# Moving the store of batch 28 behind the last load in a streaming mixture of softmaxes

## Chip, cores, metric

One core of a Trainium2 chip. DVE is the vector engine (VectorE), ACT the scalar engine (ScalarE); SP (SyncE) issues the large transfers, and the DMA engines carry them out. The metric is the device time of one execution in microseconds (us); the number of a kernel is the median of its runs. A profiled run also has a "span", from its first to its last instruction, which is about 1.8 us shorter than the device time; times inside a trace count from the start of the span.

## The reference

Logits are [32 batches, 128 rows, 4 heads, 4096], all float32: 268 MB in, 67 MB out.

```python
prior_probs = softmax(prior, axis=-1)              # [32, 128, 4]
softmax     = softmax(logits, axis=-1)             # over the 4096 entries
mixture     = np.sum(prior_probs[..., None] * softmax, axis=2)
```

## The kernel before

One batch is 8 MB of logits, held in one of two `ltile` buffers. ACT takes the exponential of each head and its row sum; DVE turns the sum into a coefficient and scales or accumulates. The result is 2 MB per batch. It lies in one of two `acc` buffers, and for batches 30 and 31 in the logits' own tile. Batches 30 and 31 are loaded in four pieces, one per head; the last batch is stored in two halves.

```python
    def load(b):
        lt = lpool.tile([P, H, V], FP32, name="ltile")       # two buffers
        n = pieces(b)                                        # 1 for b >= 30, else 4
        for h in range(0, H, n):
            nc.sync.dma_start(out=lt[:, h : h + n], in_=logits[b, :, h : h + n, :])
        ltiles[b] = lt

    def store(b, lo=0, hi=V):
        nc.sync.dma_start(out=out[b, :, lo:hi], in_=accs[b][:, lo:hi])
    # ... load(0), load(1); prior to probabilities: small, at the start ...
    for b in range(B):
        last = b == B - 1
        inplace = b >= B - 2
        # ... lt, acc ...
        for h in range(H):
            split = last and h == H - 1
            et = lt[:, h] if inplace else epool.tile([P, V], FP32, name="etile")
            nc.scalar.activation(et, lt[:, h], AF.Exp, accum_out=dsum)        # L98
            nc.vector.reciprocal(rden, dsum)                                  # L101
            nc.vector.tensor_mul(coeff, rden, pp[:, h, b : b + 1])            # L102
            if h == 0:
                nc.vector.tensor_scalar_mul(out=acc, in0=et, scalar1=coeff)   # L104
            elif not split:
                nc.vector.scalar_tensor_tensor(                               # L106
                    out=acc, in0=et, scalar=coeff, in1=acc, op0=ALU.mult, op1=ALU.add)
            else:
                ...  # last head of batch 31: four quarters (L112), a half store after two
        if b + 2 < B:
            load(b + 2)
        if not last:
            store(b)
```

All these transfers are issued by SP, in this order, into one queue. For the end that is: load 29, store 27, load 30, store 28, load 31, store 29, store 30, two halves of store 31.

The softmax here doesn't subtract the row's maximum and nothing guards it: scores larger than these inputs give would overflow.

## Time and profile before

| | before |
|---|---|
| device time, median of the first 3 runs | 785.83 us (784.52 to 786.05) |
| span of the profiled run | 783.7 us |
| bytes moved | 335.68 MB, 428 GB/s over the span |
| DVE, ACT busy | 70%, 60% |

The DMA-issuing queue of SP, kernel before, from 705 us on (start, duration, what):

```profile
710.70 1.80 SPq L45 DMA_DIRECT2D ltile<-in_logits_dram  x4
716.47 0.34 SPq L51 DMA_DIRECT2D out_dram<-acc  x1
734.89 1.79 SPq L45 DMA_DIRECT2D ltile<-in_logits_dram  x4
740.66 0.34 SPq L51 DMA_DIRECT2D out_dram<-acc  x1
757.68 19.31 SPq L51 DMA_DIRECT2D out_dram<-ltile  x3
```

These are load 30, store 28, load 31, store 29, and then three stores merged into one line. So store 28 is ahead of load 31 and store 29 already is behind it.

DVE in batch 31, kernel before (start, duration, what; in brackets the idle time before and what ended it):

```profile
757.95 2.35 DVE L104 TENSOR_SCALAR ltile<-ltile,coeff 128x4096 f32<-128x4096 f32 x1
761.52 0.16 DVE L101 RECIPROCAL rden<-dsum 128x1 f32<-128x1 f32 x1 [1.22 <-ACT ltile L98]
...
771.75 4.87 DVE L112 SCALAR_TENSOR_TENSOR ltile<-ltile,coeff 128x1024 f32<-128x1024 f32 x4
```

DVE waits 1.22 us in this batch, for an exponential that itself waited for its piece of load 31, and ends at 776.62.

The same kernel at its end, in windows of 2 us (columns: window, length, busy us of DVE, ACT and POOL, TensorE clock, DMA share, GB/s; a packet counts in the window where it starts, so a full window can read a little over 1):

```profile
768.00:770.00 2.00, 2.00 (x1) 2.00 (x1) 0.00 (x0) 1.00 0.96 410
770.00:772.00 2.00, 1.93 (x4) 1.33 (x2) 0.00 (x0) 1.00 1.03 442
772.00:774.00 2.00, 2.00 (x2) 0.00 (x0) 0.00 (x0) 1.00 0.58 246
774.00:776.00 2.00, 2.00 (x3) 0.00 (x0) 0.00 (x0) 1.00 0.63 262
776.00:778.00 2.00, 0.63 (x1) 0.00 (x0) 0.00 (x0) 1.00 1.02 422
778.00:780.00 2.00, 0.00 (x0) 0.00 (x0) 0.00 (x0) 1.00 1.00 418
```

There is a hole in the DMA share between 772 and 776 us, and this is what a reordering would hope to fill.

One more reading needs the packet and completion records. Every large transfer has 16 completions, one from each DMA engine (the records do not say which; that it is the same engine that comes last each time is inferred from its lag, which stays the same from one transfer to the next for long stretches). In this run the first of them and the last lie 4.2 us apart for load 29 (714.53 and 718.74). The Trainium skill, "DMA: Bandwidth & Descriptors", section "Why a DMA increments its semaphore by 16 and not by 1", says that the engines of one DMA finish independently and that only the full count means that all data has landed; the trace agrees, with that 4.2 us. So the DMA share is a mean over 16 engines that are not at the same place in the queue.

### The profile page before, as it was taken

The numbers are of one execution on the slowest core, as the hardware profiler recorded it, in microseconds if no ns is written. First come the engines' busy times: TensorE is split into PE (matmuls) and PEld (weight loads), VectorE is DVE, ScalarE is ACT, GpSimd is POOL, SyncE is SP. The second block draws the span as 40 slices with busy tenths as digits, with TensorE's granted clock in tenths as the row PEclk, the third lists the DMA queues.
The fourth block names the chain that finished last, engine by engine and source line by source line (L and its number), as shares of the span: only waits on it lengthen the run. The fifth ranks groups of instructions, "written<-read, shape, count | busy, mean of one in ns | idle before, by whom it ended". The sixth has DMA issues, their size and how long they took to land.

```text
span 783.7 us, 1001 instructions
## 1 busy us (share of the span) xinstructions
DVE 547.5 (70%) x408; ACT 472.7 (60%) x258; POOL 0.2 (0%) x4
## 2 busy tenths in 40 slices
DVE  3588568766687666786666866668756687666996
ACT  0776555775557755567555576555765557755963
POOL 0000000000000000000000000000000000000000
DMA  9999999999999999999999999999999999999997
GB/s 378 428 462 421 438 429 399 457 428 428 428 425 436 451 445 435 420 421 447 429 428 425 431 456 442 435 428 404 456 432 428 428 429 438 458 432 403 430 430 317
DMA packets 10280, 335.68 MB, mean 428 GB/s; under 512 B 1152, under 2 KB 1152, under 8 KB 1184
## 3 DMA queue, kind: packets, MB, share of 16 engines
q1 hardware_dynamic: 10224, 335.55, 99.4%
q10 hardware_dynamic: 48, 0.07, 0.0%
q14 instruction: 8, 0.07, 0.0%
HBM read 268.50 MB, written 67.11 MB: 428 GB/s over the span
## 4 chain that ended last, share of the span: by engine, by line
DMA 66%; ACT 14%; DVE 12%; issue 6%; DVEq 0%; SPq 0%; ACTq 0%
DMA ltile<-in_logits_dram 62%; ACT etile L98 14%; DVE acc L106 10%; DMA out_dram<-acc 4%; DVE ltile L106 1%; DVE rden L101 1%; ACT ltile L98 0%; DVE ltile L112 0%; DVE coeff L102 0%; DVE acc L104 0%; DVEq L147 0%; SPq L45 0%; ACTq L98 0%; DVEq L104 0%
## 5 line engine op out<-in xcount | busy, mean ns | idle before, releaser
L98 ACT ACTIVATE etile<-ltile 128x4096 f32<-128x4096 f32 x120 | 433.4, 3612 | 280.0 <-DMA ltile<-in_logits_dram 240.7
L106 DVE SCALAR_TENSOR_TENSOR acc<-etile,coeff,acc 128x4096 f32<-128x4096 f32 x90 | 403.6, 4485 | 3.2
L101 DVE RECIPROCAL rden<-dsum 128x1 f32<-128x1 f32 x128 | 20.5, 160 | 186.9 <-ACT etile L98 182.5
L104 DVE TENSOR_SCALAR acc<-etile,coeff 128x4096 f32<-128x4096 f32 x30 | 70.6, 2353 | 22.2 <-DMA out_dram<-acc 22.1
L98 ACT ACTIVATE ltile<-ltile 128x4096 f32<-128x4096 f32 x8 | 28.9, 3609 | 7.2 <-DMA ltile<-in_logits_dram 7.2
L102 DVE TENSOR_TENSOR coeff<-rden,pp 128x1 f32<-128x1 f32 x128 | 20.4, 159 | 4.4
L106 DVE SCALAR_TENSOR_TENSOR ltile<-ltile,coeff 128x4096 f32<-128x4096 f32 x5 | 22.4, 4485 | 0.2
L98 ACT ACTIVATION_READ_ACCUMULATOR etile<-ltile 128x1 f32 x120 | 22.4, 186 | 0.0
L60 DVE TENSOR_REDUCE pmax<-pr 32x128 f32<-32x512 f32 x1 | 0.7, 674 | 11.3 <-DMA pr<-in_prior_dram 11.3
L64 ACT ACTIVATE pe<-pc 32x512 f32<-32x512 f32 x1 | 0.6, 628 | 10.2 <-DVE pc L62 10.2
L112 DVE SCALAR_TENSOR_TENSOR ltile<-ltile,coeff 128x1024 f32<-128x1024 f32 x4 | 4.9, 1280 | 0.0
L104 DVE TENSOR_SCALAR ltile<-ltile,coeff 128x4096 f32<-128x4096 f32 x2 | 4.7, 2353 | 0.1
L64 ACT ACT_TABLE_LOAD x1 | 1.3, 1283 | 1.2 <-PEq L136 1.2
L78 DVE STREAM_TRANSPOSE pp<-pn 32x32 f32<-32x32 f32 x16 | 1.9, 169 | 0.1
L98 ACT ACTIVATION_READ_ACCUMULATOR ltile<-ltile 128x1 f32 x8 | 1.5, 186 | 0.0
L66 DVE TENSOR_REDUCE psum<-pe 32x128 f32<-32x512 f32 x1 | 0.7, 675 | 0.7 <-ACT pe L64 0.7
L71 DVE TENSOR_TENSOR pn<-pe,prec 32x512 f32<-32x512 f32 x1 | 1.0, 1020 | 0.0
L68 DVE RECIPROCAL prec<-psum 32x128 f32<-32x128 f32 x1 | 0.9, 942 | 0.0
L62 DVE TENSOR_TENSOR pc<-pr,pmax 32x512 f32<-32x512 f32 x1 | 0.7, 680 | 0.0
L136 POOL MEMSET const-bfloat16-1.0<- 128x1 bf16 x1 | 0.1, 101 | 0.0
L136 POOL MEMSET const-uint8-127<- 128x1 uint8 x1 | 0.1, 101 | 0.0
L136 POOL MEMSET const-float32-0.0<- 128x1 f32 x1 | 0.1, 98 | 0.2 <-issue 0.2
(1 smaller groups left out, 0.1 us busy)
## 6 DMA issues: line engine op xcount, KB each, us to landing
out_dram<-acc SPq DMA_DIRECT2D x30, 2048.0 KB, 31.3
ltile<-in_logits_dram SPq DMA_DIRECT2D x8, 2048.0 KB, 24.6
out_dram<-ltile SPq DMA_DIRECT2D x1, 2048.0 KB, 20.4
out_dram<-ltile SPq DMA_DIRECT2D x2, 1024.0 KB, 6.3
ltile<-in_logits_dram SPq DMA_DIRECT2D x30, 32.2
pr<-in_prior_dram ACTq DMA_DIRECT2D x1, 64.0 KB, 10.5
```

What stands on the lines that cost most here:

```text
L60: nc.vector.reduce_max(pmax, pr, axis=AX.X)
L62: nc.vector.tensor_sub(pc, pr, pmax.unsqueeze(2).to_broadcast([B, S, H]))
L64: nc.scalar.activation(pe, pc, AF.Exp)
L68: nc.vector.reciprocal(prec, psum)
L71: nc.vector.tensor_mul(pn.rearrange("b h s -> b s h"), pe, prec.unsqueeze(2).to_broadcast([B, S, H]))
L78: nc.vector.transpose(pp[32 * t : 32 * (t + 1), h, :], pn[:, h, 32 * t : 32 * (t + 1)])
L98: nc.scalar.activation(et, lt[:, h], AF.Exp, accum_out=dsum)
L101: nc.vector.reciprocal(rden, dsum)
L102: nc.vector.tensor_mul(coeff, rden, pp[:, h, b : b + 1])
L104: nc.vector.tensor_scalar_mul(out=acc, in0=et, scalar1=coeff)
L106: nc.vector.scalar_tensor_tensor(out=acc, in0=et, scalar=coeff, in1=acc, op0=ALU.mult, op1=ALU.add)
L112: nc.vector.scalar_tensor_tensor(out=acc[:, cs], in0=et[:, cs], scalar=coeff, in1=acc[:, cs], op0=ALU.mult, op1=ALU.add,)
```

## The change

Intent: the last load, load 31, should not stand behind stores; let it arrive sooner, let the stores run while the last batch is computed, and so shorten the tail.

```diff
         if b + 2 < B:
             load(b + 2)
-        if not last:
+        if b < B - 4:
+            store(b)
+        elif b == B - 3:
+            store(b - 1)
+            store(b)
+        elif b == B - 2:
             store(b)
```

The edit rewrites where the stores of the last four batches stand, but of these only store 28 changes places: stores 29, 30 and 31 were behind load 31 before.

## The prediction

> **What bounds the kernel.** The DMA engines. The slice view shows them at 9 tenths in 39 of 40 slices; 335.7 MB at 428 GB/s is the whole 783.7 us span. DVE (70%) and ACT (60%) wait: the table of waits gives 240.7 us of ACT waiting for logits. Loads and stores share one queue (q1, 99.4%). The Trainium skill, "DMA: Bandwidth & Descriptors", section "Queues, rings and completion order", says that each DMA engine consumes its ring in order. The trace agrees: landings in order, one 2 MB transfer each 4.87 us: load 29 at 718.7, store 27 at 723.6, load 30 in four pieces to 743.1, store 28 at 748.0, load 31's pieces at 752.9, 757.8, 762.7 and 767.5, store 29 at 772.4, store 30 at 778.0, the halves of store 31 at 780.5 and 782.9.
>
> The 16 engines do not run level. The packet records and the completions of each DMA show nine engines about 4.2 us ahead of the last one, and a load counts as landed only with its last engine. That engine never rests: its packets follow each other every 0.607 us up to 782.46, apart from one that took 1.06 us at 775.9. The dip of the DMA share at 772 to 775 us is the leading engines running dry until store 31 is issued at 774.26.
>
> **What the change moves.** Nothing on DVE or ACT. In the queue only store 28 passes: from before load 31 to after it. Store 29 already stood behind load 31, as did 30 and 31. Bytes are the same.
>
> Load 31's pieces land one store earlier, 4.87 us: 748.0, 752.9, 757.8, 762.7; store 28 lands at 767.5. Load 31 is still issued at 734.9 (when ACT frees its tile), about 3 us before the leading engines finish load 30, so no bubble. No acc buffer is reused after batch 29, so nothing waits for the late stores.
>
> **How much lies on the critical path.** Little. DVE limits from 723.7 on: batch 30 ends there at 757.65 in either version. Earlier data removes DVE's waits in batch 31 (1.22 us before its second head): the first head ends at 760.3, three more follow back to back (0.4 + 4.48 us each, the last 4.87 in quarters), so DVE ends at about 775.4 instead of 776.6 and store 31 is issued 1.2 us sooner. But the slowest DMA engine still has stores 29 and 30 before it until about 777.3, and it never starved before, so it drains the same bytes to about the same end. Only the 0.45 us of the stretched packet can be gained. Expected: 0 to 0.8 us less, middle 0.3.
>
> **Predicted time.** 785.5 us, 8 in 10 between 784.2 and 786.6. Faster by over 2%: 1%; within 2%: 98%; slower by over 2%: 1%.
>
> **What would show it.** Right: load 31 lands near 762.7; ACT ends near 766 instead of 771; DVE near 775.4 with no wait inside batch 31; store 28 takes about 31 us to land; the last store still lands at 782 to 783. Wrong: a DMA dip near 737 to 739 (load 31 too late for the leading engines); packets over 0.62 us in the store-only stretch after 762.
>
> **What would make it wrong.** Eight megabytes of stores in a row draining slower than 4.87 us per 2 MB; the spread among the engines changing (3.2 us until about 550 us of this run, then 4.2); a wait for a reused DMA semaphore.

## More of the kernel before

From the page of the kernel before: busy tenths of the DMA engines in 40 equal slices of the span, then what each DMA queue moved (packets, MB, share of 16 engines).

```profile
DMA  9999999999999999999999999999999999999997
DMA packets 10280, 335.68 MB, mean 428 GB/s; under 512 B 1152, under 2 KB 1152, under 8 KB 1184
q1 hardware_dynamic: 10224, 335.55, 99.4%
q14 instruction: 8, 0.07, 0.0%
```

The transfers are the whole time; only the last slice is not full.

## The result

| | before | after |
|---|---|---|
| device time, median of 4 runs | 785.88 us (784.52 to 786.05) | 786.71 us (785.89 to 787.41) |
| ratio after to before | | 1.0014, 95% interval 0.9997 to 1.0031 |
| span of the profiled run | 783.7 us | 784.6 us |

A ratio is the mean time of one kernel's runs over that of the other's runs of the same rounds, so it is not quite the ratio of the medians. The median lies 0.1 us above the predicted range and, if anything, on the slower side.

The page of the kernel after:

```profile
DMA  9999999999999999999999999999999999999997
DMA packets 10280, 335.68 MB, mean 428 GB/s; under 512 B 1152, under 2 KB 1152, under 8 KB 1184
q14 instruction: 8, 0.07, 0.0%
```

The issuing queue of SP after, from 705 us on, with loads 30 and 31 merged, then stores 28 and 29, then the last three:

```profile
711.64 25.92 SPq L45 DMA_DIRECT2D ltile<-in_logits_dram  x8
737.66 4.27 SPq L51 DMA_DIRECT2D out_dram<-acc  x2
758.60 17.74 SPq L51 DMA_DIRECT2D out_dram<-ltile  x3
```

DVE in batch 31 after, and the 2 us windows of its end:

```profile
758.87 2.35 DVE L104 TENSOR_SCALAR ltile<-ltile,coeff 128x4096 f32<-128x4096 f32 x1
761.14 0.16 DVE L101 RECIPROCAL rden<-dsum 128x1 f32<-128x1 f32 x1
...
771.10 4.87 DVE L112 SCALAR_TENSOR_TENSOR ltile<-ltile,coeff 128x1024 f32<-128x1024 f32 x4
```

```profile
770.00:772.00 2.00, 1.93 (x4) 0.00 (x0) 0.00 (x0) 1.00 0.97 418
772.00:774.00 2.00, 2.00 (x3) 0.00 (x0) 0.00 (x0) 1.00 0.69 295
774.00:776.00 2.00, 1.97 (x2) 0.00 (x0) 0.00 (x0) 1.00 0.86 356
776.00:778.00 2.00, 0.00 (x0) 0.00 (x0) 0.00 (x0) 1.00 1.05 438
778.00:780.00 2.00, 0.00 (x0) 0.00 (x0) 0.00 (x0) 1.00 0.77 320
780.00:782.00 2.00, 0.00 (x0) 0.00 (x0) 0.00 (x0) 1.00 0.23 98
```

Everything that the change was meant to do was done. DVE's wait inside batch 31 is gone, ACT has finished before 768, and the hole in the DMA share is smaller. And yet the transfers end no sooner. The landings show why; each number is the last of the 16 completions, in us from the start of the span, and in brackets from the landing of load 29:

| transfer | before | after |
|---|---|---|
| load 29 | 718.74 (0) | 719.66 (0) |
| load 30, last piece | 743.13 (24.4) | 744.08 (24.4) |
| store 28 | 748.00 (29.3) | 768.52 (48.9) |
| load 31, last piece | 767.54 (48.8) | 763.65 (44.0) |
| end of the last DVE instruction | 776.62 (57.9) | 775.97 (56.3) |
| store 29 | 772.40 (53.7) | 773.35 (53.7) |
| store 30 | 778.04 (59.3) | 778.98 (59.3) |
| store 31, second half | 782.89 (64.16) | 783.84 (64.18) |

Up to load 30 both kernels do the same; I count from load 29, which is safely before the first transfer that moves. Counted from there, load 31 lands 4.8 us sooner, DVE ends 1.6 us sooner, and the end is the same to 0.02 us. The whole 0.9 us between the two profiled spans was there before the first moved transfer.

I call the time from the landing of load 29 to the last landing "the tail". It is read within one run, the profiled one of each label, and so it is free of what happened in that run before. The totals are not: they spread by some 3 us.

### The profile page after: what moved, and what is told of

It is laid out like the page before. It is cut to its first block, busy times and chain, and to the rows that moved or that the text cites. A ratio compares the mean times of both kernels' runs of the same rounds, so it can differ in the third digit from the quotient of the medians.

```text
span 784.6 us, 1001 instructions
## 1 busy us (share of the span) xinstructions
DVE 547.3 (70%) x408; ACT 472.6 (60%) x258; POOL 0.2 (0%) x4
## 4 chain that ended last, share of the span: by engine, by line
DMA 63%; DVE 16%; ACT 13%; issue 6%; DVEq 0%; ACTq 0%; SPq 0%
DMA ltile<-in_logits_dram 59%; ACT etile L98 13%; DVE acc L106 11%; DMA out_dram<-acc 3%; DVE ltile L106 3%; DVE ltile L104 1%; DVE rden L101 1%; DVE coeff L102 1%; DVE ltile L112 0%; DVE acc L104 0%; DVEq L152 0%; ACTq L98 0%; SPq L45 0%; DVEq L104 0%
```

## The experiments

Two theories for the missing gain. D: the end is set by the slowest of the 16 DMA engines, which has work without a pause until the end, so the order of that work cannot matter. C: the end is set by the last batch's compute, and the gain there is lost to something. Beside D stands O: nothing but the bytes ever counts. For the 0.8 us by which the changed kernel was slower: S, it is scatter; R, late stores cost something.

### after_again, before_again: the two kernels, unchanged, once more

after_again:

> The changed kernel once more. Theory S (scatter): the 0.8 us by which it lay above the kernel before came from where load 29 happened to land, before the first moved store; ratio between 0.999 and 1.001, and from the landing of load 29 to the last landing 64.2 us (64.16 before, 64.18 after), with load 29 landing anywhere from 718.5 to 720. Rival R (the late stores cost something): ratio 1.001 to 1.002 again, and a tail longer than 64.2 us by some tenths.

before_again:

> The kernel before under a new label, against itself: how wide the scatter is. Both theories expect a ratio of 1.000; S expects single runs to spread over 1.5 us or more, so that after_again and this one differ by less than 0.8 us, and a tail of 64.2 us from the landing of load 29. R expects this one 0.8 us below after_again.

| | median (range), runs | ratio, 95% interval | load 29 landed | tail |
|---|---|---|---|---|
| after_again | 786.50 (784.53 to 786.65), 5 | 0.9998 (0.9984 to 1.0011) | 719.74 | 64.15 us |
| before_again | 785.81 (785.11 to 787.10), 5 | 0.9999 (0.9986 to 1.0011) | 720.35 | 64.14 us |

The ratio of 1.0014 did not come back, and the tails are equal. In before_again load 29 landed even later than in either profiled run of the changed kernel. R falls, by the tails above all: the interval of after_again by itself still reaches 1.001. S holds. That load 29 would land by 720.0 was too tight for before_again.

### light_tail: less compute in the last batch

```diff
             nc.vector.tensor_mul(coeff, rden, pp[:, h, b : b + 1])
+            if last and h == 1:
+                continue
             if h == 0:
```

> The changed kernel without one of the accumulations of batch 31 (wrong result for that batch on purpose); every transfer is unchanged. Theory D (the slowest DMA engine has work without a pause up to the end): DVE ends about 3.3 us earlier (53 us after the landing of load 29 instead of 56.3), the end stays at 64.2 us after it, ratio 0.999 to 1.002. Rival C (the end is set by the compute of the last batch): the time falls by about 3.3 us, ratio 0.996.

Ratio 0.9994 (0.9978 to 1.0009): the 3.3 us did not come, so C falls. DVE ended 53.1 us after the landing of load 29, as expected, 3.3 us sooner than in the changed kernel. But the tail was 63.39 us, not 64.2. No theory had 0.8 us of gain in it, and this led to theory F below.

### no_store28: without the store that the change moves

```diff
         elif b == B - 3:
-            store(b - 1)
             store(b)
```

> The changed kernel without the store that the change moves (batch 28 of the output is not written, wrong on purpose). Theory D: 4.87 us of work leave the slowest DMA engine, but only about 4.1 us are gained, since then the last half of store 31 is issued 56.35 us after the landing of load 29 and needs about 3.7 us more: end 60.1 us after it instead of 64.2, ratio about 0.995. Rival C: nothing, DVE ends when it ended; ratio 1.000.

Ratio 0.9961 (0.9946 to 0.9976), tail 61.23 us. The bytes count, as D says and C denies, but the tail is 1.1 us longer than I expected. The completions show where: the first of the last half store came 60.16 us after load 29, as expected, and 15 of the 16 within 0.16 us; a single engine came 0.9 us after these, 1.07 us after the first. A packet of the instruction queue had started at 777.2 us, between the landings of the two half stores. That it held this engine up is likely, not shown here.

### store29_first: the opposite order

```diff
+        if b == B - 3:
+            store(b)
         if b + 2 < B:
             load(b + 2)
-        if not last:
+        if not last and b != B - 3:
             store(b)
```

> The opposite order: the kernel before with store 29 also ahead of load 31. Theory D: load 31 lands one store later (its last piece about 53.7 us after load 29 instead of 48.8), ACT and DVE finish batch 31 about 4.8 us later (DVE about 62.7 after load 29), the DMA engines run dry before store 31, and the end comes about 2.3 us later (66.5 after load 29), ratio about 1.003. Rival O (only the bytes count, the order of the queue never does): ratio 1.000, end at 64.2.

789.22 us, ratio 1.0033 (1.0021 to 1.0046), tail 66.72 us. Now the order does matter: DVE ended 62.7 us after load 29 and the DMA engines ran dry before store 31, as these windows of store29_first show.

```profile
774.00:776.00 2.00, 2.00 (x1) 2.00 (x1) 0.00 (x0) 1.00 0.31 131
776.00:778.00 2.00, 1.93 (x4) 0.59 (x2) 0.00 (x0) 1.00 0.08 33
778.00:780.00 2.00, 2.00 (x3) 0.00 (x0) 0.00 (x0) 1.00 0.02 4
```

The last DMA work starts only after that. So O is wrong as a general rule: the order is free only as long as it leaves work on the slowest engine until DVE is done. The kernel before had that already; this one has not, and pays 2.6 us in the tail (expected 2.3).

### old_no2930, new_no2930: both orders with nothing left to hide behind

```diff
 # old_no2930, from the kernel before          # new_no2930, from the kernel after
-        if not last:                           #   elif b == B - 3:
+        if b < B - 3:                          #       store(b - 1)
             store(b)                           #   (store(b) for 29 and 30 removed)
```

> The order of before, with stores 29 and 30 left out (two batches of the output not written, wrong on purpose), so that the DMA engines have nothing left when DVE ends. Theory D: the end is now set by DVE and the last half store, about 61.7 us after the landing of load 29; ratio about 0.997. Rival O: 9.7 us less, ratio 0.9876.

> The order of after, with stores 29 and 30 left out likewise. Theory D: the gain of the reordering that was hidden now shows: end 1.6 us sooner than in old_no2930, about 60.1 us after the landing of load 29, since DVE ended 56.3 us after it in the changed kernel and 57.9 in the kernel before. Rival O: the same as old_no2930 to 0.2 us.

| | median, runs | ratio, 95% interval | tail |
|---|---|---|---|
| old_no2930 | 784.97 us, 5 | 0.9976 (0.9964 to 0.9989) | 61.89 us |
| new_no2930 | 782.40 us, 5 | 0.9949 (0.9936 to 0.9963) | 60.33 us |

The windows of old_no2930, and then those of new_no2930, with the DMA engines empty until the first half of store 31:

```profile
774.00:776.00 2.00, 2.00 (x3) 0.00 (x0) 0.00 (x0) 1.00 0.01 4
776.00:778.00 2.00, 2.00 (x2) 0.00 (x0) 0.00 (x0) 1.00 0.70 291
778.00:780.00 2.00, 0.23 (x1) 0.00 (x0) 0.00 (x0) 1.00 1.04 430
```

```profile
770.00:772.00 2.00, 1.93 (x4) 0.00 (x0) 0.00 (x0) 1.00 0.00 0
774.00:776.00 2.00, 2.00 (x2) 0.00 (x0) 0.00 (x0) 1.00 0.73 303
776.00:778.00 2.00, 0.20 (x1) 0.00 (x0) 0.00 (x0) 1.00 1.01 418
```

The hidden gain is real: 1.56 us in the tail where 1.6 were expected. The mean times differ by 2.06 us, and I do not count the rest: it lies before the tail, where the two profiled runs differ by the scatter.

### quarter_compute: a quarter of the work

```diff
-        for h in range(H):
-            split = last and h == H - 1
+        for h in (0,):
+            split = last
```

In batch 31 the quarters then scale instead of accumulating.

> The kernel before with only the first of the four heads computed (wrong on purpose); all loads and stores stay. Theory D: the stream of transfers is the whole time, so three quarters of the compute away change it by less than 1.5 us: 784 to 786, ratio 0.998 to 1.001. Rival C: the last batch's compute after its last load, about 9 us from landing to the last DVE instruction, goes as well, ratio about 0.990.

784.81 us, ratio 0.9977 (0.9965 to 0.9990), while DVE was busy 92.0 us instead of 547.5. Three quarters of the compute are worth 1.8 us, not the 8 that C expects. D missed too, by a little: it had expected less than 1.5 us and a ratio of at least 0.998. Of these, 0.8 us are in the tail (63.38 us), as in light_tail; no packet of the instruction queue fell into it. The rest lies before the tail; the interval of the ratio, 0.8 to 2.8 us, leaves room for it to be scatter.

### four_less, two_scalar_new, two_scalar_old: the packet of the instruction queue

Theory F came out of light_tail: a packet of the instruction queue that falls into the tail takes time from the slowest DMA engine. In both original kernels and both repeats one packet of 8,192 bytes of the instruction queue starts within about 1.3 us of the end of DVE's work (at 774.7 to 777.2 us), and store 30 on the last engine takes some 5.6 us where every other 2 MB takes 4.87. In the trace of the kernel before the packet runs from 775.585 to 775.894 on the slowest engine's place in the sequence, and the next data packet there takes 1.055 us instead of 0.611. (Packet records do not name their engine either; this is the chain in which each packet starts where one ended, followed back from the last.) That is 0.31 us for the packet and 0.44 for the stretch, 0.75 us in all. So this is the origin of the "stretched packet" of the prediction. In light_tail, with one DVE instruction fewer, the packet came at 783.9, after the last store, and store 30 took 4.84 us. The queues between 770 and 782 us, in the changed kernel and then in light_tail:

```profile
q1 hardware_dynamic: 412, 3.84, 76.1%
q14 instruction: 1, 0.01, 0.2%
```

```profile
q1 hardware_dynamic: 414, 3.82, 74.9%
```

The Trainium skill, "DMA: Bandwidth & Descriptors", section "Queues, rings and completion order", says that each engine takes turns between the queues that have work for it; the trace agrees as far as that the packet goes ahead of data of store 30 that was queued long before. The test is a correct kernel with a few DVE instructions fewer:

```diff
             nc.vector.reciprocal(rden, dsum)
+            two = h == 0 and b < 4          # four_less; the two_scalar kernels: h == 0
+            if not two:
+                nc.vector.tensor_mul(coeff, rden, pp[:, h, b : b + 1])
-            nc.vector.tensor_mul(coeff, rden, pp[:, h, b : b + 1])
+            if two:
+                nc.vector.tensor_scalar(out=acc, in0=et, scalar1=rden,
+                    scalar2=pp[:, h, b : b + 1], op0=ALU.mult, op1=ALU.mult)
-            if h == 0:
+            elif h == 0:
```

> The changed kernel with four VectorE instructions fewer (in batches 0 to 3 the first head is scaled by two scalars in one instruction; correct result). Theory F: the 8 KB packet of the instruction queue at 775 us is fetched when DVE nears the end of its program, and costs the slowest DMA engine 0.8 us (its store 30 took 5.6 us instead of 4.87 in all four full kernels, and 4.85 in light_tail, where the packet came at 783.9). With four instructions fewer it comes after the last store or not at all: from load 29 to the last landing 63.4 us instead of 64.2, store 30 at 4.87 us, ratio about 0.999. Rival W (the stretch comes from store 31 being issued into a busy ring): tail still 64.2.

> The changed kernel with that edit in all 32 batches: 32 VectorE instructions fewer. F: tail 63.4 us, ratio about 0.999 (0.8 us, a little more if an earlier fetch falls on another engine). W: 64.2. If the two-scalar form ran slower than 2.35 us, DVE would end later, without effect on the end.

> The same edit on the kernel before. F and D together: tail 63.4 us too, so equal to two_scalar_new within the scatter of 1 us: the order of the stores still gives nothing. If the order did matter once the fetch is gone, this would be slower than two_scalar_new by up to 1.6 us.

| | median (range), runs | ratio, 95% interval | tail |
|---|---|---|---|
| four_less | 786.21 (784.63 to 787.28), 5 | 0.9998 (0.9985 to 1.0010) | 63.40 us |
| two_scalar_new | 785.24 (784.30 to 787.76), 6 | 0.9992 (0.9978 to 1.0005) | 63.38 us |
| two_scalar_old | 786.08 (784.82 to 786.39), 5 | 0.9993 (0.9980 to 1.0006) | 63.35 us |

From the page of four_less:

```profile
span 782.7 us, 997 instructions
q14 instruction: 7, 0.06, 0.0%
```

Seven such packets instead of eight fall into the span, and the tail is 63.4 us in all three, as F expects and W does not. With the packet gone the two orders still have the same tail (63.38 and 63.35). In the totals 0.8 us cannot be seen: four_less measured 0.9998. I count this as shown by the tails alone, and none of these versions as one that beats the two kernels. Which engine's program the packet belongs to is not settled, but much points to DVE: in four_less the packets near 317, 558 and 775 us came at 341, 582 and 784, while the other five stayed within 5 us of where they are in the four full kernels. What sets the moment of its transfer stays open: in no_store28, where DVE's instructions were all there, it came 2.3 us after DVE's end, and in the two kernels without stores 29 and 30 some 3.8 us before it.

## Why the prediction was right or wrong

- **What bounds the kernel: right.** The stream of transfers. Without three quarters of the compute the time falls by 1.8 us (quarter_compute).
- **What moves: right.** Only store 28 passes load 31; no instruction changes on DVE and ACT.
- **The step from load 31 to DVE: right.** Load 31 lands 4.8 us sooner and DVE ends 1.6 us sooner, both counted from load 29; predicted were 4.87 and 1.2. No DMA hole opened before 772, and the long stretch of stores kept 4.87 us per 2 MB up to store 30, which took 5.6 us in both kernels.
- **The critical path: right.** The slowest DMA engine never starved. light_tail takes 3.3 us of DVE work from the end, and the time stays but for the 0.8 us of the instruction packet; the pair without stores 29 and 30 takes the DMA work away, and then 1.56 us appear. The Trainium skill's statement that an engine consumes its ring in order ("DMA: Bandwidth & Descriptors", section "Queues, rings and completion order") carried this step, and the landings of all runs agree with it.
- **The gain of 0 to 0.8 us, middle 0.3: wrong in its middle.** "Only the 0.45 us of the stretched packet can be gained": nothing was gained, 64.16 against 64.18 us. The stretch was not caused by the order of the stores but by the instruction packet before it, which both orders have. With that packet it costs 0.8 us.
- **The predicted time, 785.5 us, 784.2 to 786.6: this is the step that failed.** The measured median is 786.71. Of the 1.2 us in between, 0.3 is the gain that measured 0.0; the other 0.9 is the scatter of the starting point, and this is the term that was mis-sized. I took it from three runs within 1.5 us, with a median of 785.83. The 38 runs of the kernel before spread from 784.52 to 788.10, 3.6 us, with a median of 786.1 (different chips are pooled here; within one round it was 2.0 to 2.4 us); the 9 runs of the changed kernel from 784.53 to 787.41, median 786.5. Even the centre was drawn from a low sample. That the four runs came out 0.1 us above the range and not inside it is chance: five more of the same kernel, in after_again, had a median of 786.50. The prediction named "the spread among the engines changing" among the things that would make it wrong, and did not put it into the range. In the profiled runs of the four full kernels the gap between first and last engine at load 29 was 4.2, 4.9, 5.3 and 5.3 us, and load 29 landed between 718.7 and 720.4.

What stays open is why the engines drift apart differently from run to run; most of it happens in the first 250 us of each run, and no experiment here addressed it. One later step can be read from the traces, though. The prediction saw the lag of the last engine grow from 3.2 to 4.2 us at about 550 us, and there, at 557.7 to 559.4 us, the four full kernels have a packet of the instruction queue. Across it the gap between the first and the last completion of a transfer grows by 0.9 to 1.0 us in each (3.24 to 4.20, 4.01 to 4.88, 4.28 to 5.25, 4.38 to 5.34). In two_scalar_old the packet came at 607.5 us and the step with it (4.17 to 5.14 us); quarter_compute has neither (3.58 us before and after). In two_scalar_new the packet came at 608.5 us without a step, and across the packet at 316 to 318 us the gap of the four full kernels grew by 0.0, 0.7, 0.3 and 0.9 us; I take it that such a packet does not always hit the engine that is last. So a part of the drift, and perhaps of its difference from run to run, has the same origin as the 0.8 us of the tail.

## What to carry to other kernels

When transfers fill the whole span, ask of a reordering not whether the last load comes sooner, but whether the slowest DMA engine has a gap before the end; a hole in the mean DMA share can be, as here, only the faster engines waiting. For effects below the scatter of the total, measure within a run, from the last event that both kernels have in common to the end; and take the scatter from more than three runs before giving a range.

## What the Trainium skill lacked or had wrong

- "DMA: Bandwidth & Descriptors", section "Why a DMA increments its semaphore by 16 and not by 1": it says that the engines finish independently, but not by how much. Here, in a stream that is never interrupted, the first and the last engine come apart by 3.6 to 5.8 us at load 29 (0.3 to 0.7 us at the first load), different from run to run. The last one sets every landing.
- "Runtime: NRT & Kernel Launch", section "Instruction fetch mechanics": it calls the cost of crossing a block boundary "mostly hidden" and speaks of blocks of 16 KiB. Here the packets of the instruction queue, taken to be these fetches by the queue's name, are of 8,192 bytes, eight in the span. One of them in the tail made the end 0.8 us later (64.2 against 63.4 us), not by stalling the compute engine but by delaying data on one DMA engine.
- Neither of these pages says that removing a few instructions can move such a packet past the last store (774.7 us in the changed kernel, 783.8 us with four VectorE instructions fewer), or that the same packets can add 0.9 to 1.0 us to the lag of the last DMA engine in mid-run.
